# First products of 56 expert tiles instead of 48 ahead of the main loop of a sparse-expert layer

## The chip, the cores and the metric

One core of a Trainium2 chip runs the whole program. The metric is device time in microseconds of one execution, as the median of the runs shown. The engines are TensorE (PE; PEld is its weight load), VectorE (DVE), ScalarE (ACT), GpSimd (POOL) and SyncE (SP). Two queues carry nearly all transfers: the one that SP issues on (the page calls it q1, hardware_dynamic) and the one that POOL's gathers use (q0, software_dynamic). Both share 16 DMA engines.

## The reference, cut to what matters

The layer ends in an expert mixer with 16384 experts, of which each of 1024 tokens picks 8 x 16 = 128 with weights `g`:

```python
a = jnp.einsum('cd,ced->ce', hc, u[ic])          # first product, with u of the picked experts
a = jax.nn.gelu(a, approximate=False) * gc       # gate
return jnp.einsum('ce,ced->cd', a, v[ic])        # second product, with v of the picked experts
```

Before it come projections, two attentions and a memory attention, all in float32; the change touches none of them.

## The kernel before, in words

The tokens are 8 blocks of 128. Blocks 0 to 3 are done **gathered**: for each of their 128 picks POOL gathers 128 rows of `peer_u` (line 1028) or `peer_v` (line 1044), 512 KB, into one of 7 `rows` buffers, and DVE multiplies and sums one such tile (line 1031 for u, line 1050 for v). That is 4 x 2 x 128 = 1024 items, in the order U0 V0 U1 V1 U2 V2 U3 V3. Blocks 4 to 7 are done **dense**: all 16384 experts in 128 tiles of 128 experts, on PE, with a dense weight matrix `Wd` that is zero where an expert was not picked.

`dense` (line 1183) does the dense half in three pieces.

1. **Weights.** The generator `weights` (line 1109) makes `Wd` block by block: a routing (`route`, DVE), codes, and 32 units of two matmuls of codes, a compare on DVE (`ah`, line 1163), a ScalarE step (`oh`, line 1161), four matmuls and a copy to `wbuf` (line 1169). Every 16 units a `wbuf` of 4 MB is full, and 8 stores of 512 KB carry it to `Wd` in DRAM (line 1177).
2. **First products beside it.** For the tiles `e` below `early` (48), `first(e)` (line 1201) loads 512 KB of transposed `peer_u` (`uraw`, 3 buffers), splits it into two float32r parts (ACT writes the high part, line 106; DVE the low part, line 107), and makes 24 matmuls into an `acc` tile. ACT takes the Gelu (line 1217), and SP stores 256 KB as `ga[e]` in DRAM (line 1219). After the last one `pace.drain("weights")` (line 1220) issues whatever of the weights is left.
3. **The main loop**, 32 groups of four tiles. `group` (line 1232) loads `wl` from `Wd` (512 KB for two tiles, line 1237), takes `c` either from `ga` (line 1241, one buffer of 256 KB) or by a fresh `first(e)` and a Gelu (line 1244), multiplies them on DVE (line 1245) and splits the product (ACT and DVE, lines 106 and 107). `second` (line 1251) loads and splits four tiles of `peer_v` (line 1256) and makes 8 sets of 12 matmuls; four sets stay in PSUM (`kept`), four are added to `accu` by DVE (line 1274). So groups 0 to 11 load their `c`, and groups 12 to 31 make it.

The order is set in two steps. `Pace` (line 44) interleaves the generators: each `first` ticks 8 x 3 x 0.216 = 5.184 us and each of the 8 sets of a `second` ticks 2.592 us, and the lane of the gathered items issues one item per `u_each` of ticks (1.3 beside the weights, 2.0 in the main loop, `U_EACH`). Then a list scheduler at build time gives each engine a fixed order by priority: the gathered items stand 3000 instructions behind the place where they were issued (`EXPERT_LAG`), so they fill DVE where the dense work leaves it free. Every engine and the SP queue then run their list strictly in order.

The pools matter too. `gelu`, `wbuf` and the rest of the weights' tiles lie in pool `wb`, which closes before pool `sp` (`wl`, `c`, `v`, `vraw`, `accu`) opens in the same place; and PSUM is laid out anew between them (4 `acc` buffers before, 2 after, beside the four `kept`).

Of the kernel before, what the change touches and what calls it, by code (L numbers as in the profile page):

```python
# [78 lines left out]
class K:  # L79
# [1103 lines left out]
    def dense(self, psum, early):  # L1183
# [5 lines left out]
        with ExitStack() as ctx:  # L1189
# [11 lines left out]
            def first(e):  # L1201
                uT = load_u(e)
                o = self.acc()
                for k in range(KD):
                    self.mm3(o, [u[:, k] for u in uT], [x[:, k] for x in h3], k == 0, k == KD - 1)
                self.pace.tick(KD * 3 * 0.216)
                return o

            ga = {}
            with ExitStack() as c2:  # L1210
                self.wb = c2.enter_context(self.pool("wb"))
                self.u_each = U_EACH[-2]
                self.pace.add("weights", self.weights(blks))
                for e in range(early):
                    o = first(e)
                    t = self.wb.tile([P, 512], F32, name="gelu", bufs=2)
                    nc.scalar.activation(t, o, AF.Gelu)
                    ga[e] = self.scratch([P, 512], f"ga{e}")
                    nc.sync.dma_start(ga[e], t)
                self.pace.drain("weights")  # L1220
            self.route_ctx.close()
            psum = self.psum_phase(psum, "ps3", A_BUFS)
            kept = {}
# [72 lines left out]
    def run(self, ctx):  # L1296
# [74 lines left out]
        psum = self.psum_phase(psum, "ps2", D_BUFS)  # L1371
        psum = self.dense(psum, EARLY)
        self.pace.drain("experts")
        psum.close()


EARLY = 48
V_AHEAD, V_EACH = 0, None
ORDER = [("U", 0), ("V", 0), ("U", 1), ("V", 1), ("U", 2), ("V", 2), ("U", 3), ("V", 3)]
ROWS_T, LOADS_T, FILL_EACH, FILL_LAG = (5, 4), (2, 2), (0.7, 2.4), 100  # L1380
# [5 lines left out]
KEEP, A_BUFS, O_BUFS = 4, 2, 2  # L1386
U_BUFS, V_BUFS = 3, (4, 4, 4)
SELECT_EACH = (5.0, 7.0)
U_EACH, ROUTE_EACH = (1.9, 1.8, 1.9, 1.3, 2.0), 3.0
ROUTE_LAG, EXPERT_LAG = 300, 3000  # L1390
_INS = ["x", "mem", "positions", "norm_mix_g", "w_in", "da_lambda", "da_subln_g", "w_branch_a", "w_branch_b", "gate_bias",
        "w_out", "norm_mem_g", "mem_kv_norm_g", "w_mem_q", "w_mem_kv", "w_mem_o", "norm_ffn_g", "peer_w_q",
# [29 lines left out]
```

## Time and profile before

| | us |
|---|---|
| median of 3 runs | 3506.32 (3500.16 to 3507.83) |
| the profiled execution, its time | 3504.34 |
| its span, first to last instruction | 3502.6 |
| PE busy | 3011.4 |
| DVE busy | 2853.1 |

So 1.7 us of the profiled execution lie outside its span, and it is 2.0 us below the median. Stretches of the trace are given in us from the span's start. The weights and the first products beside them run from about 1640 to 2198, the main loop from 2242 to the end.

### The profile page before, as it was taken

The numbers are of one execution on the slowest core, as the hardware profiler recorded it, in microseconds if no ns is written. First come the engines' busy times: TensorE is split into PE (matmuls) and PEld (weight loads), VectorE is DVE, ScalarE is ACT, GpSimd is POOL, SyncE is SP. The second block draws the span as 40 slices with busy tenths as digits, with TensorE's granted clock in tenths as the row PEclk, the third lists the DMA queues.
The fourth block names the chain that finished last, engine by engine and source line by source line (L and its number), as shares of the span: only waits on it lengthen the run. The fifth ranks groups of instructions, "written<-read, shape, count | busy, mean of one in ns | idle before, by whom it ended". The sixth has DMA issues, their size and how long they took to land. (4 is left out here: it accounts for less than half of the span.)

```text
span 3502.6 us, 42276 instructions
## 1 busy us (share of the span) xinstructions
PE 3011.4 (86%) x13234; PEld 2283.0 (65%) x13234; DVE 2853.1 (81%) x6623; ACT 1398.2 (40%) x2537; POOL 1389.4 (40%) x1122
## 2 busy tenths in 40 slices
PE   8999888798687698676899895588899999999997
PEld 7777766553355575455677674466677888787886
DVE  6656554598878979888999888677789999899998
ACT  5756344245666441322546465222222222222222
POOL 0010000011245246653122665424457665777665
PEclk9999989899899799788999998799999999999999
DMA  4575544335799579897486999999999999999997
GB/s 138 163 186 133 169 138 142 124 121 192 210 296 297 143 262 362 296 327 277 149 296 219 364 377 346 369 302 319 307 340 368 380 381 367 364 364 387 376 381 285
DMA packets 394210, 964.64 MB, mean 275 GB/s; under 512 B 36713, under 2 KB 146049, under 8 KB 392577
## 3 DMA queue, kind: packets, MB, share of 16 engines
q0 software_dynamic: 155264, 560.01, 45.3%
q1 hardware_dynamic: 238720, 401.94, 33.7%
q8 instruction: 104, 1.70, 0.2%
q14 instruction: 122, 0.99, 0.1%
HBM read 871.64 MB, written 90.18 MB: 275 GB/s over the span
## 5 line engine op out<-in xcount | busy, mean ns | idle before, releaser
L1028 POOL DMA_INDIRECT rows<-in_peer_u_dram,ii x512 | 673.8, 1316 | 920.8 <-DVE rows L1031 377.0
L1044 POOL DMA_INDIRECT rows<-in_peer_v_dram,ii x512 | 651.0, 1272 | 438.9 <-DVE h3s L1050 286.2
L1050 DVE SCALAR_TENSOR_TENSOR h3s<-rows,wexp,h3s 128x1024 f32<-128x1024 f32 x508 | 651.1, 1282 | 38.9 <-DMA rows<-in_peer_v_dram,ii 29.4
L1031 DVE SCALAR_TENSOR_TENSOR rows<-rows,h3s 128x1024 f32<-128x1024 f32 x512 | 611.9, 1220 | 81.5 <-DMA rows<-in_peer_u_dram,ii 80.0
L129 PE MATMUL acc<-fT,uT 128*128 128x512 f32 x1024 | 415.7, 406 | 46.3 <-ACT uT L106 26.0
L131 PE MATMUL acc<-fT,uT 128*128 128x512 f32 x1024 | 413.5, 404 | 11.8 <-DVE uT L107 11.5
L130 PE MATMUL acc<-fT,uT 128*128 128x512 f32 x1024 | 410.2, 401 | 0.0
L106 ACT ACTIVATE c<-wl 128x512 fp32r<-128x512 f32 x128 | 80.2, 631 | 817.1 <-PE out L130 407.8
L143 POOL TENSOR_TENSOR rstd<-msq,mhalf 128x1 f32<-128x1 f32 (+1 forms) x42 | 35.6, 847 | 597.4 <-DVE msq L141 578.6
L129 PEld LDWEIGHTS acc<-fT,uT 128*128 128x128 f32 x1024 | 197.0, 192 | 92.2 <-ACT uT L106 26.8
L131 PEld LDWEIGHTS acc<-fT,uT 128*128 128x128 f32 x1024 | 197.0, 192 | 66.7 <-DVE uT L107 21.0
L130 PE MATMUL kept<-v,c 128*128 128x512 f32 x512 | 206.2, 405 | 38.8 <-DVE v L107 38.8
L129 PE MATMUL kept<-v,c 128*128 128x512 f32 x512 | 202.6, 402 | 37.6 <-ACT v L106 36.2
L106 ACT ACTIVATE uT<-uraw 128x1024 fp32r<-128x1024 f32 x128 | 135.5, 1059 | 245.4 <-PE acc L130 135.0
L130 PEld LDWEIGHTS acc<-fT,uT 128*128 128x128 f32 x1024 | 197.2, 193 | 39.2
L107 DVE TENSOR_TENSOR w<-wraw,w 128x512 fp32r<-128x512 f32 (+1 forms) x176 | 116.7, 680 | 117.9 <-ACT w L106 111.2
L129 PE MATMUL out<-v,c 128*128 128x512 f32 x512 | 203.9, 398 | 9.7 <-DVE accu L1274 9.7
L131 PE MATMUL kept<-v,c 128*128 128x512 f32 x512 | 203.4, 397 | 0.0
L130 PE MATMUL out<-v,c 128*128 128x512 f32 x512 | 203.0, 396 | 0.0
L131 PE MATMUL out<-v,c 128*128 128x512 f32 x512 | 202.8, 396 | 0.0
L562 ACT ACTIVATE junk<-W,xb 128x384 bf16<-128x384 f32 (+5 forms) x186 | 163.8, 881 | 77.3 <-DVE xb L560 67.8
L127 PE MATMUL acc<-wraw,hT 128*128 128x512 f32 (+1 forms) x384 | 168.4, 592 | 14.1 <-ACT tok L349 10.9
(361 smaller groups left out, 6691.5 us busy)
## 6 DMA issues: line engine op xcount, KB each, us to landing
uraw<-in_peer_ut_dram SPq DMA_DIRECT2D x128, 512.0 KB
vraw<-in_peer_v_dram SPq DMA_DIRECT2D x128, 512.0 KB
Wd<-wbuf SPq DMA_DIRECT2D x64, 512.0 KB
wl<-Wd SPq DMA_DIRECT2D x64, 512.0 KB
wraw<-in_w_in_dram SPq DMA_DIRECT2D x40, 512.0 KB
fraw<-in_w_in_dram SPq DMA_DIRECT2D x32, 512.0 KB
wraw<-in_w_out_dram SPq DMA_DIRECT2D x24, 512.0 KB
ga<-gelu SPq DMA_DIRECT2D x48, 256.0 KB
```

The costliest lines, as they stand in the source:

```text
L106: self.nc.scalar.activation(hi, src, AF.Copy)
L107: self.last_dve = self.nc.vector.tensor_tensor(lo, src, hi.bitcast(F32), op=OP.subtract).ins
L127: self.last_pe = nc.tensor.matmul(out, l[0], r[0], start=start, stop=stop).ins
L129: nc.tensor.matmul(out, l[0], r[0], start=start, stop=False)
L130: nc.tensor.matmul(out, l[0], r[1], start=False, stop=False)
L131: self.last_pe = nc.tensor.matmul(out, l[1], r[0], start=False, stop=stop).ins
L143: nc.gpsimd.tensor_tensor(r, v, self.mhalf[:, :n], op=OP.pow)
L562: nc.scalar.activation(junk[:, :(b + 1) * P], self.W[b], AF.Sign, bias=xb[:, j:j + 1].bitcast(F32), accum_out=s[:, j:j + 1])
L1028: nc.gpsimd.indirect_dma_start(out=u, out_offset=None, in_=a["peer_u"][0], in_offset=bass.IndirectOffsetOnAxis(ap=ii[:, j:j + 1], axis=0))
L1031: nc.vector.scalar_tensor_tensor(u, u, 1.0, h3, op0=OP.mult, op1=OP.mult, accum_out=aa[:, j:j + 1])
L1044: nc.gpsimd.indirect_dma_start(out=v, out_offset=None, in_=a["peer_v"][0], in_offset=bass.IndirectOffsetOnAxis(ap=r["ii"][:, j:j + 1], axi ...
L1050: nc.vector.scalar_tensor_tensor(o, v, w[:, j:j + 1], o, op0=OP.mult, op1=OP.add)
```

## The change

It makes and stores the first products of 56 tiles instead of 48, so that groups 12 and 13 load their `c` as well. `drain("weights")` stays where it was, behind tile 47; the eight further tiles come behind it, inside the same loop and before the pool `wb` closes. And the pace of the gathered items in the main loop is 1.95 instead of 2.0.

```diff
@@ -1217,7 +1217,8 @@
                     nc.scalar.activation(t, o, AF.Gelu)
                     ga[e] = self.scratch([P, 512], f"ga{e}")
                     nc.sync.dma_start(ga[e], t)
-                self.pace.drain("weights")
+                    if e == BESIDE - 1:
+                        self.pace.drain("weights")
             self.route_ctx.close()
@@ -1374,7 +1375,7 @@
-EARLY = 48
+EARLY, BESIDE = 56, 48
@@ -1386,7 +1387,7 @@
-U_EACH, ROUTE_EACH = (1.9, 1.8, 1.9, 1.3, 2.0), 3.0
+U_EACH, ROUTE_EACH = (1.9, 1.8, 1.9, 1.3, 1.95), 3.0
```

## Rows read from the trace of the kernel before

**Rows 1.** The page's busy times, and its 40 slices of the span (87.6 us each), in tenths.

```profile
PE 3011.4 (86%) x13234; PEld 2283.0 (65%) x13234; DVE 2853.1 (81%) x6623; ACT 1398.2 (40%) x2537; POOL 1389.4 (40%) x1122
...
PE   8999888798687698676899895588899999999997
...
DVE  6656554598878979888999888677789999899998
```

**Rows 2.** Busy time of each engine in five stretches: the end of the weights, the passage to the main loop, the main loop up to group 11 (4th product of group 0 to 4th product of group 11), groups 12 to 30, and the end. Columns: stretch, length, busy us of the engines (instructions), granted TensorE clock, DMA share, GB/s.

```profile
2118.00:2198.00 80.00, 56.17 (x342) 43.92 (x343) 74.47 (x91) 54.88 (x70) 49.66 (x41) 0.88 0.92 335
2198.00:2242.00 44.00, 10.09 (x45) 8.05 (x44) 24.28 (x22) 4.88 (x7) 19.08 (x18) 0.66 1.03 392
...
2255.00:2549.00 294.00, 242.50 (x950) 190.39 (x949) 225.66 (x308) 67.69 (x90) 106.02 (x87) 0.91 0.92 310
2549.00:3443.00 894.00, 870.77 (x3774) 713.04 (x3773) 847.15 (x1036) 244.78 (x318) 596.65 (x434) 0.99 0.99 370
3443.00:3502.60 59.60, 41.03 (x180) 33.31 (x178) 50.42 (x51) 12.58 (x19) 26.76 (x22) 0.88 0.74 264
```

**Rows 3.** The same columns for two stretches of 100 us, one where the gathered items are v and one where they are u.

```profile
2800.00:2900.00 100.00, 100.00 (x443) 82.80 (x442) 98.66 (x96) 27.23 (x35) 66.12 (x50) 1.00 1.02 382
3100.00:3200.00 100.00, 95.70 (x414) 78.45 (x413) 91.82 (x142) 28.69 (x37) 72.28 (x50) 0.98 0.98 363
```

**Rows 4.** PE in order of time around the passage: first and last of the 48 matmuls of tiles 48 and 49, and the first matmuls of group 0. Columns: start, us, engine, line, what; in brackets the idle time before it and what ended it.

```profile
2196.69 0.47 PE L129 MATMUL acc<-fT,uT 128*128 128x512 f32 x1
...
2207.47 0.39 PE L131 MATMUL acc<-fT,uT 128*128 128x512 f32 x1
2241.77 0.79 PE L129 MATMUL kept<-v,c 128*128 128x512 f32 x1 [33.91 <-ACT v L106]
2242.36 0.63 PE L129 MATMUL out<-v,c 128*128 128x512 f32 x1
...
2245.88 0.43 PE L129 MATMUL out<-v,c 128*128 128x512 f32 x1
```

**Rows 5.** The SP queue in order of time from 2116 to 2245: its transfers as issued, in its fixed order.

```profile
2116.64 0.33 SPq L1196 DMA_DIRECT2D uraw<-in_peer_ut_dram  x1
2118.46 0.33 SPq L1219 DMA_DIRECT2D ga<-gelu  x1
2120.49 0.33 SPq L1196 DMA_DIRECT2D uraw<-in_peer_ut_dram  x1
2164.78 43.63 SPq L1177 DMA_DIRECT2D Wd<-wbuf  x16
2208.51 6.34 SPq L1196 DMA_DIRECT2D uraw<-in_peer_ut_dram  x2
2214.95 1.16 SPq L1237 DMA_DIRECT2D wl<-Wd  x1
2216.16 5.05 SPq L1241 DMA_DIRECT2D c<-ga  x1
```

**Rows 6.** The DMA queues from 2198 to 2242: packets, MB, share of the 16 engines.

```profile
q0 software_dynamic: 2454, 8.92, 51.6%
q1 hardware_dynamic: 4206, 8.30, 51.4%
...
rows<-in_peer_v_dram,ii POOLq DMA_INDIRECT x18
```

**Rows 7.** DVE in order of time: the product of the gate and the weights of a tile (line 1245), first of group 0, then the 4th of groups 0, 11 and 30.

```profile
2237.51 0.69 DVE L1245 TENSOR_TENSOR wl<-c,wl 128x512 f32<-128x512 f32 x1 [10.02 <-DMA c<-ga]
...
2255.04 0.69 DVE L1245 TENSOR_TENSOR wl<-c,wl 128x512 f32<-128x512 f32 x1 [1.37 <-DMA c<-ga]
...
2549.07 0.69 DVE L1245 TENSOR_TENSOR wl<-c,wl 128x512 f32<-128x512 f32 x1 [1.39 <-DMA c<-ga]
...
3442.84 0.68 DVE L1245 TENSOR_TENSOR wl<-acc,wl 128x512 f32<-128x512 f32 x1
```

**Rows 8.** DVE's groups of instructions from 2255 to 2549 (groups 1 to 11): count, busy us, mean ns, and the idle time before them with what ended it.

```profile
L1031 DVE SCALAR_TENSOR_TENSOR rows<-rows,h3s 128x1024 f32<-128x1024 f32 x56 | 66.3, 1220 | 2.8 <-DMA rows<-in_peer_u_dram,ii 2.8
...
L1050 DVE SCALAR_TENSOR_TENSOR h3s<-rows,wexp,h3s 128x1024 f32<-128x1024 f32 x29 | 37.1, 1280 | 0.1
L1245 DVE TENSOR_TENSOR wl<-c,wl 128x512 f32<-128x512 f32 x44 | 30.4, 692 | 62.7 <-DMA c<-ga 37.3 <-DMA wl<-Wd 17.6 <-issue 7.5
```

**Rows 9.** The same from 2549 to 3443 (groups 12 to 30).

```profile
L1050 DVE SCALAR_TENSOR_TENSOR h3s<-rows,wexp,h3s 128x1024 f32<-128x1024 f32 x232 | 297.4, 1282 | 10.0 <-DMA rows<-in_peer_v_dram,ii 5.3
L1031 DVE SCALAR_TENSOR_TENSOR rows<-rows,h3s 128x1024 f32<-128x1024 f32 x200 | 237.4, 1221 | 35.9 <-DMA rows<-in_peer_u_dram,ii 35.0 <-DMA h3s<-h 0.7
...
L107 DVE TENSOR_TENSOR uT<-uraw,uT 128x1024 fp32r<-128x1024 f32 x76 | 92.5, 1217 | 0.9 <-ACT uT L106 0.9
...
L1048 DVE TENSOR_SCALAR h3s<-rows,wexp 128x1024 f32<-128x1024 f32 x2 | 1.5, 753 | 0.1
```

**Rows 10.** Who waited for whom on PE from 2549 to 3443: us in total, times, longest.

```profile
PE acc L129 <- DVE wl L1245: 20.2, 10, 4.3
```

## The prediction

> **What bounds the kernel now.** I read the page's busy times and slices first, for where engines stand idle together; then the table by stage; then PE, SP and DVE in order of time around the one hole that the table shows; last the groups of instructions of the main loop's two halves. In the slices PE and DVE are near 9 only from slice 30 on [rows 1]. In the table [rows 2] the reader is to see three regimes. From 2549 on PE has 871 of 894 us and DVE 847: both are nearly full, and which one sets the pace changes with the gathered items: with v items PE is full and DVE at 98.7, with u items both have holes [rows 3], the largest of PE's being 20.2 us behind DVE's product [rows 10]. From 2255 to 2549, where groups load their `c`, PE has 242 of 294 us and DVE 226; DVE waits 62.7 us at line 1245, 37.3 of them for the single `c` buffer's load [rows 8]. And from 2198 to 2242 PE has 10 of 44 us and DVE 24 [rows 2]: PE ends tile 49 at 2207.7 and starts group 0 33.9 us later [rows 4]. In that passage the transfers are what is late. SP stood from 2121 to 2165 waiting for a `wbuf` to fill, then pushed 16 stores in 43.6 us, two loads of `uraw`, and only at 2215 the first `wl` [rows 5]; the gathers and SP's queue each took 51% of the 16 engines, 392 GB/s together [rows 2, 6]. The first product of group 0 ran at 2237.5, after DVE had waited 10.0 us for its `c` [rows 7].
>
> **The change, part by part.** The sum is against the profiled execution, 3504.34 us; the median is 2.0 higher.
>
> (a) *Groups 12 and 13 change kind.* A group that loads took (2549.07 - 2255.04) / 11 = 26.7 us, one that makes its `c` (3442.84 - 2549.07) / 19 = 47.0 [rows 7]. Two of them: 2 x 20.3 = 40.6 us less. This counts everything these groups lose (8 `uraw` loads, 8 splits on ACT and DVE, 192 matmuls) and gain (8 `c` loads in the one-buffer chain), and it counts the gathered items that go with them, for which see (c).
>
> (b) *The eight first products come ahead of group 0.* PE needs 11.0 us for two [rows 4], so 44.0 for eight. The hole is 33.9, so PE alone would start group 0 10.1 later; that is the lower end, if tiles 56 and 57 are run ahead into the two `acc` buffers as 48 and 49 were. Past the SP queue go 8 loads of 0.52 MB and 8 stores of 0.26 MB, 6.3 MB, ahead of `wl`. If they only add to the common 392 GB/s they cost 16.0 us; at the rate that SP's queue itself had, 8.30 MB in 44 us = 189 GB/s [rows 6], 33.3, the upper end. I take 13, between PE's 10.1 and 16.0: two of the loads already stand ahead of the stores [rows 5], and SP has 44 empty us there for one more. In the hole PE falls to its lower clock: the granted clock of the stretch is 0.66 [rows 2], and the first matmuls of group 0 stand 0.44 us apart against 0.23 before it [rows 4], some 2 us over the ten of them. A filled hole gives these back: -2.
>
> The eight Gelus (ACT is at a third or less in the main loop [rows 2]) cost nothing; their cover is ACT's idle time, and if it went they would delay only the stores, 0.6 us each. The passage adds one wait: SP's store of `ga` waits for its Gelu, and queued behind it are the loads of `wl`, `c` and `vraw` that group 0 waits for; that is the slower rival below.
>
> (c) *The gathered items lose their place.* A group that loads carried 85 / 11 = 7.7 items, one that makes carried (232 + 2 + 200) / 19 = 22.8 [rows 8, 9]. Two that change kind drop 30.2 items. A passage 13 us longer takes 13 x 18 / 44 = 5.3 of them at the rate the gathers had there [rows 6]; 24.9 are left, at 1.28 us [rows 9] 31.9 us of DVE. Nothing hides them in full: where items are v, DVE is at 98.7 of 100 [rows 3]. Against them stand DVE's 10.0 us at the first `c` [rows 7], which eight first products give the load time to cover, and u items that move out of the late groups, where each waits (35.0 / 200) 0.17 us for its rows, against 0.05 in the groups that load [rows 8, 9]: two more such groups with some ten u items each, 2.4 us. I take 31.9 - 12.4 = 19.5. The bounds are 0 (the late groups' 47 us of DVE idle [rows 2] take all) and 31.9.
>
> (d) *The pace.* The eight firsts tick 41.5 us, so 31.9 items are issued ahead of the main loop; its ticks fall from 1078 to 1037 us, at 1.95 instead of 2.0, so 532 instead of 539 items. The list thus runs out 24 items, about one group, sooner. POOL's queue gets these gathers earlier, but each waits for a `rows` buffer that DVE frees, and DVE's order is filled by what room the dense work leaves: 22 to 24 items in a late group, 8 in a loading one, not the 20.7 and 10.4 that the pace of 2.0 asks for [rows 8, 9]. I take 0; ends -5 (the end of the list no longer trails the last group) and +5.
>
> Sum: -40.6 + 13 - 2 + 19.5 + 0 = -10.1. The profiled execution would take 3494.2, the median 3496.2.
>
> **A rule that speaks against it.** In the passage both queues are always pending and share evenly, 51.6 against 51.4% [rows 6]. The Trainium skill, "DMA: Bandwidth & Descriptors", section "Queues, rings and completion order", says that each DMA engine takes turns between the queue rows with work, a packet at a time. By it SP's queue could not get more than its even share while gathers are waiting, (b) would be 33.3 and not 13, and the sum +10 before the longer passage is credited with its items; the trace agrees with the even split, but not that gathers are pending all through a longer passage, which no run here shows.
>
> **The rivals.**
>
> *No change.* Follow DVE instead of PE. Its work is the same in both kernels, so only its idle time counts: from 2198 on 19.7 us in the passage, 68.3 in the groups that load, 46.9 after, 9.2 at the end [rows 2]. Two more groups of the loading kind add 2 x 6.2 = 12.4; two fewer of the other kind save 2 x 2.5 = 4.9; the passage keeps its 20, since gathers there come every 44 / 18 = 2.4 us. Net +7 at most, and -3 if the 10.0 us at the first `c` go: 3503 to 3513. For it: DVE's 98.7 [rows 3]. Against it: PE's waits for DVE in the late groups are only 20 us [rows 10].
>
> *Slower: SP's queue.* The eighth `ga` store stands ahead of the first `wl`, and from the issue of that `wl` to group 0 took 2241.8 - 2215.0 = 26.8 us [rows 4, 5], with 16 stores just ahead. If SP's list has the loads of group 0 behind the last Gelu, the hole is not filled but pushed behind the eight: (b) is 33 instead of 13. The longer passage takes 13.5 items, 16.7 are left, 21 us. Sum: -40.6 + 33 + 21 = +13, 3519. It decides the sign once group 0 starts later than 2241.8 + 20.
>
> *Much faster.* All items find room: -40.6 + 10.1 + 0 = -30, 3476. Against it rows 3.
>
> *The change doesn't do what it says.* PE has 24 idle us in the weights' last 80 [rows 2]; the builder may order the eight into these gaps instead of behind the last unit. DVE is at 74.5 of 80 there, so eight splits of 1.22 [rows 9] push its items out, and the hole stays with its wait for the stores. (b) is then 0 to 5, but the 10.0 us of (c) stay: -40.6 + 3 + 29 = -9, the same time by another way; it is counted with the forecast.
>
> **How the numbers follow.** About 0.2% (7 us) is what a measurement of this kernel can tell from no change. The forecast (3485 to 3499) has 0.36, with the last rival in it; much faster 0.08; no change 0.34; slower 0.22. So faster 0.44, same 0.34, slower 0.22. The likeliest case's own range is 3485 to 3499; to leave out no more than 2 in 10 the range reaches into the faster case to 3480 and over the slower one's 3519, to 3520.
>
> **What would show it.** Right: group 0's first matmul between 2250 and 2260 with a hole of under 10 us before it, groups 12 and 13 at some 27 us, and groups 14 to 30 at 47 to 49. PE's hole behind tile 55 still over 25 us: the SP rival. Late groups at 49 us or more with DVE at 98% and PE's waits for DVE's product well over 20 us: no change. It is wrong altogether if stretches before 2118 move by more than a few us, since nothing in the sum touches them, or if the loading groups slow from 26.7 because more u items fall into them.

## The result, and the profile after

The median went from 3504.7 us (4 runs) to 3529.2 us (4 runs, 3521.5 to 3534.6): a ratio of 1.0058, 95% interval 1.0036 to 1.0080, which is 13 to 28 us slower. I had forecast 3496 with a range of 3480 to 3520, and gave slower 0.22. The profiled execution of after, the shortest of its four, took 3521.47 us with a span of 3519.7, so the two profiles show 17 us of the 24 between the medians.

The busy times and the PE and DVE slices of after, to be laid beside [rows 1]:

```profile
PE 3011.1 (86%) x13234; PEld 2279.9 (65%) x13234; DVE 2855.8 (81%) x6623; ACT 1395.1 (40%) x2537; POOL 1370.1 (39%) x1122
...
PE   8999888798687698686899889788889999999991
...
DVE  6656444698878889888999789687789999899997
```

The instructions are as many on every engine, and PE's, DVE's and ACT's busy times are the same to about 3 us. PE's hole behind the weights is smaller (slices 25 and 26 were 5 and 5, now 9 and 7) and PE's last slice fell from 7 to 1, while DVE goes on at 7. The table by stage of after, to compare with [rows 2] (columns as there; the stretches begin and end at the same marks of the program):

```profile
2118.00:2198.00 80.00, 77.08 (x463) 59.54 (x462) 75.25 (x93) 60.58 (x79) 45.27 (x38) 1.00 0.94 350
2198.00:2245.00 47.00, 27.54 (x109) 21.48 (x107) 28.27 (x24) 8.82 (x11) 19.95 (x18) 0.81 1.03 395
2256.00:2548.00 292.00, 244.69 (x977) 193.41 (x976) 224.99 (x302) 67.81 (x90) 103.93 (x86) 0.93 0.92 317
2548.00:2610.00 62.00, 50.16 (x193) 39.43 (x192) 45.91 (x71) 12.19 (x16) 25.24 (x19) 0.89 0.88 297
2610.00:3404.00 794.00, 777.26 (x3374) 637.09 (x3373) 757.00 (x935) 220.07 (x286) 526.24 (x387) 0.99 1.00 372
3404.00:3447.00 43.00, 42.90 (x190) 35.08 (x188) 42.37 (x39) 6.85 (x10) 30.16 (x26) 1.00 0.88 309
3447.00:3519.70 72.70, 0.30 (x2) 0.00 (x0) 52.53 (x47) 5.63 (x10) 31.11 (x31) 0.52 0.74 276
```

The last four stretches in before, cut at the 4th product of groups 13 and 31 and at PE's last matmul:

```profile
2549.00:2625.00 76.00, 73.47 (x316) 60.20 (x315) 70.60 (x108) 21.61 (x28) 44.97 (x34) 0.97 0.94 339
2625.00:3443.00 818.00, 797.30 (x3460) 652.84 (x3459) 776.54 (x929) 223.18 (x290) 551.67 (x401) 0.99 1.00 373
3443.00:3483.60 40.60, 40.60 (x179) 33.30 (x178) 36.90 (x37) 9.13 (x13) 23.32 (x19) 1.00 0.85 305
3483.60:3502.60 19.00, 0.43 (x2) 0.01 (x1) 13.52 (x15) 3.45 (x6) 3.44 (x3) 0.63 0.48 174
```

Read the lengths: 76 became 62, 818 became 794, and the end behind PE's last matmul went from 19.0 to 72.7. There DVE's busy time is 52.5 where it was 13.5.

The eight first products stand mostly inside the weights' drain: PE starts six of them between 2114 and 2195 and the other two by 2206. Tiles 56 and 57 then run ahead of group 0, as 48 and 49 did in before; the matmuls at 2228.59 to 2236.72 are tile 57's. PE's waits ahead of group 0, beside [rows 4]:

```profile
2228.59 0.79 PE L129 MATMUL acc<-fT,uT 128*128 128x512 f32 x1 [11.52 <-ACT uT L106]
...
2236.72 0.39 PE L131 MATMUL acc<-fT,uT 128*128 128x512 f32 x1
2245.15 0.80 PE L129 MATMUL kept<-v,c 128*128 128x512 f32 x1 [8.04 <-ACT v L106]
2245.74 0.63 PE L129 MATMUL out<-v,c 128*128 128x512 f32 x1
2246.17 0.63 PE L129 MATMUL kept<-v,c 128*128 128x512 f32 x1
```

SP's queue over the same time, beside [rows 5]; seven of the eight stores of `ga` are out by 2210, before, between or right behind the stores of `wbuf`, the eighth at 2223.65:

```profile
2155.86 0.33 SPq L1219 DMA_DIRECT2D ga<-gelu  x1
2158.14 0.33 SPq L1196 DMA_DIRECT2D uraw<-in_peer_ut_dram  x1
2162.59 9.24 SPq L1177 DMA_DIRECT2D Wd<-wbuf  x8
...
2197.44 9.08 SPq L1177 DMA_DIRECT2D Wd<-wbuf  x8
2206.62 2.98 SPq L1219 DMA_DIRECT2D ga<-gelu  x2
...
2223.65 0.32 SPq L1219 DMA_DIRECT2D ga<-gelu  x1
2224.06 0.86 SPq L1196 DMA_DIRECT2D uraw<-in_peer_ut_dram  x2
2225.02 0.40 SPq L1238 DMA_DIRECT2D wl<-Wd  x1
```

The 4th products of groups 0, 11, 13 and 31 on DVE, beside [rows 7] (group 13 stood at 2625.27 in before, group 31, the last, at the 3442.84 shown there):

```profile
2256.07 0.69 DVE L1246 TENSOR_TENSOR wl<-c,wl 128x512 f32<-128x512 f32 x1 [0.43 <-DMA c<-ga]
...
2547.79 0.69 DVE L1246 TENSOR_TENSOR wl<-c,wl 128x512 f32<-128x512 f32 x1 [1.41 <-DMA c<-ga]
...
2609.81 0.69 DVE L1246 TENSOR_TENSOR wl<-c,wl 128x512 f32<-128x512 f32 x1 [1.29 <-DMA c<-ga]
...
3404.06 0.69 DVE L1246 TENSOR_TENSOR wl<-acc,wl 128x512 f32<-128x512 f32 x1 [0.17 <-ACT acc L1245]
```

And the end on DVE, in order of time from PE's last matmul (3446.91) on; below it the last item and the last instruction of before:

```profile
3447.94 27.70 DVE L1050 SCALAR_TENSOR_TENSOR h3s<-rows,wexp,h3s 128x1024 f32<-128x1024 f32 x21
...
3489.89 1.28 DVE L1050 SCALAR_TENSOR_TENSOR h3s<-rows,wexp,h3s 128x1024 f32<-128x1024 f32 x1 [2.81 <-DMA rows<-in_peer_v_dram,ii]
3492.40 1.28 DVE L1050 SCALAR_TENSOR_TENSOR h3s<-rows,wexp,h3s 128x1024 f32<-128x1024 f32 x1 [1.23 <-DMA rows<-in_peer_v_dram,ii]
3493.72 1.22 DVE L1063 TENSOR_TENSOR rows<-rows,h3s 128x1024 f32<-128x1024 f32 x1
...
3514.81 1.28 DVE L148 SCALAR_TENSOR_TENSOR uraw<-uraw,rstd,vraw 128x1024 f32<-128x1024 f32 x1 [0.73 <-POOL rstd L143]
```

```profile
3492.47 1.28 DVE L1050 SCALAR_TENSOR_TENSOR h3s<-rows,wexp,h3s 128x1024 f32<-128x1024 f32 x1
...
3497.64 1.28 DVE L148 SCALAR_TENSOR_TENSOR rows<-rows,rstd 128x1024 f32<-128x1024 f32 x1 [0.73 <-POOL rstd L143]
```

PE is done 37 us sooner, but the last gathered item starts at 3492.40, in before at 3492.47. Behind it come the finish of gathered block 3 and the finishes of the four dense blocks (a finish adds the residual, normalizes and stores a block); in before the dense finishes began among the items. Items behind group 31's products: 56, in before 22.

### The profile page after: what moved, and what is told of

Read it like the earlier page. It is cut to its first block, busy times and chain, and to the rows that moved or that the text cites. A ratio compares the mean times of both kernels' runs of the same rounds, so it can differ in the third digit from the quotient of the medians.

```text
span 3519.7 us, 42272 instructions
## 1 busy us (share of the span) xinstructions
PE 3011.1 (86%) x13234; PEld 2279.9 (65%) x13234; DVE 2855.8 (81%) x6623; ACT 1395.1 (40%) x2537; POOL 1370.1 (39%) x1122
## 4 chain that ended last, share of the span: by engine, by line
PE 31%; DVE 20%; issue 19%; DMA 15%; POOL 10%; ACT 5%; SPq 0%; POOLq 0%; ACTq 0%; DVEq 0%
POOL rows L1028 6%; PE acc L129 4%; PE acc L130 4%; PE acc L131 4%; POOL rows L1044 4%; DMA c<-ga 3%; DMA rows<-in_peer_u_dram,ii 3%; PE po L720 2%; DVE h3s L1050 2%; DVE rows L1031 2%; DMA rows<-in_peer_v_dram,ii 2%; DMA so<-pq 2%; PE fill L127 1%; PE acc L127 1%; PE out L1167 1%
## 5 line engine op out<-in xcount | busy, mean ns | idle before, releaser
L1028 POOL DMA_INDIRECT rows<-in_peer_u_dram,ii x512 | 666.1, 1301 | 947.1 <-DVE rows L1031 407.7
L1044 POOL DMA_INDIRECT rows<-in_peer_v_dram,ii x512 | 643.5, 1257 | 451.2 <-DVE h3s L1050 291.7
L1050 DVE SCALAR_TENSOR_TENSOR h3s<-rows,wexp,h3s 128x1024 f32<-128x1024 f32 x508 | 651.4, 1282 | 37.1 <-DMA rows<-in_peer_v_dram,ii 26.9
```

The costliest lines, as they stand in the source:

```text
L1028: nc.gpsimd.indirect_dma_start(out=u, out_offset=None, in_=a["peer_u"][0], in_offset=bass.IndirectOffsetOnAxis(ap=ii[:, j:j + 1], axis=0))
L1044: nc.gpsimd.indirect_dma_start(out=v, out_offset=None, in_=a["peer_v"][0], in_offset=bass.IndirectOffsetOnAxis(ap=r["ii"][:, j:j + 1], axi ...
L1050: nc.vector.scalar_tensor_tensor(o, v, w[:, j:j + 1], o, op0=OP.mult, op1=OP.add)
```

## The experiments

Times are medians; ratios are against runs of before on the same chip, in brackets the 95% interval. All profiles begin to differ by some us in the stages that nothing touches (the first split of `uT`, with which the weights' stage begins, starts between 1631 and 1645), so stages are compared by their lengths.

**Is it the pace?** The change also set the pace from 2.0 to 1.95. One run undoes that, one does it alone.

```
e1_pace20 (of after):      U_EACH[-1]  1.95 -> 2.0
e2_pace_only (of before):  U_EACH[-1]  2.0  -> 1.95
```

> The changed kernel with the pace of the gathered items back at 2.0. Theory (order of the finishes): the main loop's ticks, 1036.8 us, still issue 518 items at 2.0, and only 511 are left behind the eight, so the list still runs out inside the loop, the finish of gathered block 3 is still issued ahead of the finishes of the dense blocks, and ScalarE's and DVE's lists still hold those back behind the last item: the tail of 20 us stays, 3520 to 3532, like the changed kernel. Rival (the pace of 1.95 itself costs the time): back to the kernel before, 3500 to 3508.

> The kernel before with the pace 1.95 alone, 48 early tiles. Theory (order of the finishes): 1078.3 us of ticks issue 553 items and only 542 are left, so the list runs out inside the loop and the four dense finishes queue up behind the gathered one; PE ends near 3485 as before, the last item near 3485 to 3490, then about 20 us of finishes one after the other: 3508 to 3518. Rival (the eight tiles cost the time, not the pace): within 5 us of the kernel before.

e1: 3534.0, ratio 1.0088 [1.0064, 1.0112], 2 us above the range of its theory. e2: 3505.3 in 10 runs (3491 to 3525), 1.0004 [0.9986, 1.0022], as its rival had it. The pace alone is worth nothing that can be measured, and undoing it in after gives nothing back; term (d) stands.

**Is it the order of the finishes at the end?** In after the finish of the gathered block 3 stands ahead of the dense ones, which then run one behind the other for 20 us. e3 issues it behind them; e4 lets the list of items outlast the loop. (The edits are cut to what matters, here and below.)

```
e3_held:     gathered_v, block 3:  self.held = (b, o); return   # instead of finish
             run, after the drain: self.finish(*self.held, ...)
e4_pace205:  U_EACH[-1]  1.95 -> 2.05
```

> The changed kernel, with the finish of gathered block 3 held back and issued behind the dense finishes. Theory: the last item stays near 3494, since DVE's work sets it, but the dense finishes run between PE's end (3447) and 3475, and only one finish of 6 to 9 us comes behind the last item: 3498 to 3508, equal to the kernel before, with PE done 35 us earlier. Rival (the tail is slow because its gathers are, not for the order): within 5 us of the changed kernel, 3520 or more.

> The changed kernel with the pace at 2.05: 1036.8 / 2.05 = 506 items are issued in the loop and 511 are left, so the list does not run out and the last finish is issued behind the dense ones, with no other edit. Theory (order of the finishes): as e3, 3498 to 3508. Rival (a thinner pace lets more items pile up behind PE's end): slower than the changed kernel, 3530 or more.

e3: 3522.4, 1.0059 [1.0038, 1.0080]. e4: 3526.0, 1.0068 [1.0044, 1.0093]. The theory fell (e4 lies below its rival's 3530, too). In e3's trace the dense finishes do run among the items, and the last item starts at 3517.8 instead: the finishes cost their time in either place.

**Is it the number of items?** The last 36 v items of block 3 left out, in after and in before, each with block 3's finish held as in e3.

```
e5_held_short, e6_before_held_short:  for j in range(P - 36 if b == NG - 1 else P)
```

> The changed kernel with the finish of gathered block 3 held back as before, and the last 36 of its 128 v items left out (the sums of block 3 lack them). Theory (DVE's ledger: with the eight tiles PE is done 35 to 40 us early and what is left is the items that had no place, one after the other at 1.3 us): 36 x 1.32 = 47 us less than the held kernel's 3522, 3470 to 3482, and PE ends again near 3450 to 3460. Rival (PE and its finishes still set the end): within 10 us of 3522.

> The kernel before with the same two edits: the last 36 v items of block 3 left out. Theory (DVE's ledger): in the kernel before PE and the items end together, so PE's end near 3484 and the finishes behind it hold the time: 3490 to 3502, at most 10 us less than the kernel before. Rival (items set the end there too): 3455 to 3465.

e5: 3472.1, 0.9896 [0.9871, 0.9921], 50 us under e3. e6: 3499.9, 0.9987 [0.9976, 0.9997], 2 us under before. Both as expected: items set the end of after, while in before PE's dense work is late enough to hide 36 of them. With 36 items fewer in both, the change gains 28 us (3472.1 against 3499.9), so PE's gain is real; the items eat it.

**DVE's additions, or the gathers?** An item is both, so e5 could not tell. e13 leaves the last 36 gathers and cuts their additions to 8 columns; e14 leaves the additions and takes the gathers away. Both are edits of after with the finish held.

```
e13: scalar_tensor_tensor(o[:, :8], v[:, :8], ...)        # last 36 items
e14: if not last 36:  v = self.rows(); indirect_dma_start(out=v, ...)
```

> The kernel after with block 3's finish held (as in the run named held), and of the last 36 v items of block 3 only the gathers stay: their DVE additions are cut from 1024 columns to 8, so their sums are incomplete in the other columns. 36 x 1.28 = 46 us of DVE work leave, no gather does. DVE theory (DVE's work alone sets the end): 3470 to 3484, as when both were left out (3472.1). Gathers theory (behind PE's end GpSimd issues the gathers back to back, one per 1.02 + 0.30 = 1.32 us, and DVE follows them): 3510 to 3522, against 3522.35 with all of it. Something between, 3490 to 3505: DVE sets the pace up to PE's end and the gathers behind it.

> The other half of the same test: the last 36 v items of block 3 keep their full DVE additions but have no gather of their own (they add the last gathered rows again, so the sums of block 3 are other ones). 36 x 1.32 = 47.5 us of GpSimd's issuing and 18.9 MB of transfers leave, no DVE work does. DVE theory: 3510 to 3522. Gathers theory, and one by which the transfers' bytes set the end (18.9 MB at 372 GB/s are 51 us): 3470 to 3484. In between, 3490 to 3505: the two limit together.

e13: 3520.8, 1.0063 [1.0044, 1.0082]. e14: 3521.8, 1.0058 [1.0039, 1.0077]; 10 runs each, against 3522.4 for e3. Taking away either half alone is worth nothing, both together 50 us. The stretch behind PE's end, first e13, then e14 (columns as in the table by stage):

```profile
3453.00:3516.60 63.60, 0.46 (x3) 0.03 (x1) 14.88 (x40) 3.45 (x6) 30.37 (x32) 0.55 0.83 308
```

```profile
3458.00:3521.40 63.40, 0.69 (x4) 0.23 (x2) 52.71 (x45) 3.45 (x6) 3.52 (x3) 0.54 0.11 41
```

Same length, 63.6 and 63.4 us, with DVE busy 14.9 in one and 52.7 in the other, and 308 against 41 GB/s. What each runs at, GpSimd's gathers in e13 and DVE's additions in e14, in order of time:

```profile
3496.72 0.94 POOL L1044 DMA_INDIRECT rows<-in_peer_v_dram,ii  x1 [0.30 <-issue]
3497.96 0.93 POOL L1044 DMA_INDIRECT rows<-in_peer_v_dram,ii  x1 [0.30 <-issue]
```

```profile
3470.46 39.58 DVE L1051 SCALAR_TENSOR_TENSOR h3s<-rows,wexp,h3s 128x1024 f32<-128x1024 f32 x30
3510.08 1.22 DVE L1067 TENSOR_TENSOR rows<-rows,h3s 128x1024 f32<-128x1024 f32 x1
```

A gather takes GpSimd 1.24 us (the starts' distance), an addition 39.58 / 30 = 1.32 us of DVE, alone on its engine in both cases. So behind PE's end an item costs 1.3 us twice, side by side, and only fewer items make it shorter. That the two lengths agree so well is partly chance: in e13 the dense finishes stand among the last gathers, and GpSimd waits 5.2 and 2.3 us for DVE's part of two of them.

**How does it go with the number of early products?** e11 and e15 make 64 and 40 of them; e12 moves the drain, so that all 56 stand beside the weights.

```
e11_early64:         EARLY, BESIDE = 64, 48      # of after
e12_beside56:        EARLY, BESIDE = 56, 56      # of after
e15_before_early40:  EARLY = 40                  # of before
```

> The changed kernel with 64 early tiles instead of 56, so that groups 14 and 15 load their c too. Theory (DVE's ledger): PE ends another 25 to 40 us earlier, some 30 more items are left behind its end, two more loading groups add 10 us of DVE idle time and the longer tail some 3 to 5: 3538 to 3548. Rival (the 25 us are a fixed price of breaking the order at the passage): 3500 to 3525, the 40 us of PE coming back.

> The changed kernel with the weights drained behind all 56 tiles, as the loop of the kernel before does with its 48: the same work, the eight not behind the drain but beside it. Theory (DVE's ledger: where PE does the eight is of no account): within 8 us of the changed kernel, 3520 to 3537. Rival (the place behind the last unit is what costs, by its loads and stores at the passage): back to 3500 to 3512.

> The kernel before with 40 early first products, not 48: the change run backwards. Theory of two ends (PE's dense work and the items end together in the kernel before; whichever is later sets the time): PE's end moves back by 2 x 20.3 = 40.6 us and the items gain room, so PE sets the end: 3530 to 3548. Rival (what more early products cost comes on top whatever PE does, so fewer of them gain): 3478 to 3495.

e11: 3555.8, 1.0145 [1.0121, 1.0169], 8 us above what I expected. e12: 3521.0, 1.0059 [1.0038, 1.0081]: where the eight are put does not matter, as expected. In e12's trace PE's hole is back, and group 0 starts 626.9 us behind the first split instead of 606.2:

```profile
2269.29 0.79 PE L129 MATMUL kept<-v,c 128*128 128x512 f32 x1 [34.48 <-ACT v L106]
```

PE ends 13.7 us later than in after by that measure, and the end behind it is 50.4 us instead of 72.4: PE's later end costs nothing.

e15: 3502.3, 1.0007 [0.9986, 1.0028], a miss for both theories. I had PE's end moved back by 40.6 us, but the weights' stage became 46 us shorter too (434.4 instead of 480 us from the first split to 80 us ahead of the last `wbuf`) and the passage behind it 12 us, while PE's main loop became only 31 us longer; PE ended 27 us sooner against the first split, and 16 items started behind its end (3 in before). So before does not stand at a sharp crossing; from 40 to 48 the time is flat, and by the ratios it rises by about 20 us to 56 and by 30 more to 64.

One row of each tells why: the stretch from the first split of `uT` to the end, in the order 40, 48 (before), 56 (after), 64:

```profile
1640.00:3501.10 1861.10, 1665.16 (x7496) 1337.20 (x7496) 1656.29 (x2935) 638.77 (x826) 970.92 (x732) 0.95 0.91 331
```

```profile
1637.00:3502.60 1865.60, 1659.84 (x7496) 1330.39 (x7496) 1654.88 (x2935) 639.33 (x825) 969.14 (x732) 0.95 0.91 333
```

```profile
1638.90:3519.70 1880.80, 1658.61 (x7496) 1328.09 (x7496) 1658.04 (x2935) 637.32 (x825) 949.05 (x732) 0.95 0.91 332
```

```profile
1641.70:3567.70 1926.00, 1674.77 (x7496) 1340.14 (x7494) 1660.60 (x2936) 636.93 (x825) 952.50 (x732) 0.93 0.90 327
```

DVE's busy time is 1655 to 1661 in all four; what is left of the length, its idle time, is 204.8, 210.7, 222.8 and 265.4. In e11 the second eight don't fit into the drain: its passage is 103 us long with DVE at 71.5 of it, and two more groups wait for their `c`. (e11's profiled execution is 14 us over its median.)

**Two ways to make items cheaper or waits fewer.** A second `c` buffer should end the 37.3 us of [rows 8]; and GpSimd could take a quarter of the late groups' splits of `v` off DVE.

```
e7 (of before), e8 (of after, finish held):  name="c", bufs=1 -> 2
e9 (of after), e10 (of before), from group 14 on, last tile of a group:
   nc.scalar.activation(vv[0], raw, AF.Copy)
   nc.gpsimd.tensor_tensor(vv[1], raw, vv[0].bitcast(F32), op=OP.subtract)
```

> The kernel before with two buffers for the loaded c instead of one. Theory (DVE's idle time counts one for one): DVE's 50 us of waiting for c's load and part of the 18 for wl go, 20 to 45 us less: 3455 to 3482. Rival (the loading groups are held by the transfers, or by PE): within 7 us of the kernel before.

> The changed kernel with two buffers for the loaded c and the finish of gathered block 3 held back. Theory (DVE's ledger): 56 loads now go unwaited for, 25 to 50 us less than the held kernel's 3522, and the eight tiles then cost no more than 5 us against the kernel before with two buffers: 3460 to 3495. Rival (transfers hold the loading groups): within 7 us of 3522.

> The changed kernel with one of the four v splits of each group from 14 on taken from DVE and given to GpSimd (18 subtractions of 128x1024). Theory (DVE's ledger: behind PE's end DVE still has 36 items, so DVE's work counts one for one): 18 x 1.14 = 20 us of DVE go, 17 items fewer behind PE's end, 3502 to 3514 against 3529 for the changed kernel. Rival (GpSimd's own queue or the gathers set the end): within 7 us of 3529, or slower, as its subtraction delays gathers.

> The kernel before with the same 18 subtractions given to GpSimd. Theory (PE and DVE end together there): PE's end near 3484 holds the time, at most 8 us less: 3492 to 3502. Rival (DVE alone sets the end before, too): 3480 to 3487.

The theory missed in all four. e7: 3507.9, 1.0010 [0.9996, 1.0025], as its rival had it; e8: 3536.6, 1.0079 [1.0054, 1.0105], outside both, though not clear of e3's 1.0059. DVE's waits in e7's loading groups (total us, times, longest):

```profile
DVE wl L1245 <- DMA wl<-Wd: 29.4, 6, 8.2
DVE wl L1245 <- issue: 12.0, 3, 6.0
DVE wl L1245 <- DMA c<-ga: 11.4, 5, 4.0
DVE accu L1274 <- PE out L131: 9.6, 10, 2.0
```

The wait mostly changed its name: for `c` 11.4 instead of 37.3, for `wl` 29.4 instead of 17.6, at "issue" 12.0 instead of 7.5 [rows 8], and for PE's `out` 9.6 instead of 2.5. A second buffer of `c` alone does not shorten these groups.

e9: 3545.7, 1.0112 [1.0086, 1.0139], slower, as its rival allowed; e10: 3518.2, 1.0055 [1.0034, 1.0076], outside both. The splits of `v` that stay on DVE, from 2620 to 3420, in after and in e9 (count, busy us, mean ns):

```profile
L107 DVE TENSOR_TENSOR v<-vraw,v 128x1024 fp32r<-128x1024 f32 x72 | 84.1, 1218 | 0.0
```

```profile
L107 DVE TENSOR_TENSOR v<-vraw,v 128x1024 fp32r<-128x1024 f32 x52 | 95.5, 1877 | 0.0
...
L1260 POOL TENSOR_TENSOR v<-vraw,v 128x1024 fp32r<-128x1024 f32 x18 | 44.2, 2455 | 5.9 <-ACT v L1259 5.6
```

Twenty splits fewer stand in the window (18 of them on GpSimd), and the others take 11.4 us more than all 72 did; the last section shows how.

## Why the prediction was wrong, point by point

(a) *Two groups change kind*: right. From group 0's first matmul to its last matmul, PE took 1241.8 us in before and 1201.8 in after, 40.0 less; I had 40.6. By the 4th products, groups 12 and 13 took 30.0 and 32.0 us, more than my 27. Group 14 took 27.9 instead of 47.9, as group 12 took 27.1 in before: two of its first products stand ahead of group 0.

(b) *The eight ahead of group 0*: mis-sized. I had +13 - 2; against the first split, group 0's first matmul moved by 1.4 us (604.8 to 606.2). My last rival described it: the eight went into the gaps of the drain, where PE is now busy for 77.1 of 80 us instead of 56.2, and of the 33.9 us of the passage some 20 are still idle (11.5 and 8.0 above). The 6.3 MB cost nothing that shows. The -2 for the clock did not come: behind the hole of 8.0 us group 0's first matmuls stand 0.43 us apart again, and the granted clock from 2245.1 to 2250.0 is 0.50, the lower of the two levels. The Trainium skill's rule that a DMA engine takes turns between the queues with work ("DMA: Bandwidth & Descriptors", "Queues, rings and completion order"), by which (b) would have been 33.3, did not decide. The shares were even again, 52.3 and 50.6% from 2198 to 2245, but most of the transfers had gone out earlier instead of waiting in the passage. The slower rival had the right sign and the wrong mechanism.

(c) *The gathered items*: the step that failed. I took 31.9 us for 24.9 items and credited 12.4; the end behind PE's last matmul grew by 53.8 us against the 19.5 of the term. Three things were wrong in it. First, 34 more items were left behind group 31's products (56 against 22), not 24.9. Groups 12 to 14 carried 31 instead of 59, near my 30.2, but no longer passage took any: up to group 0's 4th product 478 items were done, in before 483, with eight more splits on DVE ahead of group 0. Second, the credits: the wait for the first `c` went from 10.0 to 1.2 us, but DVE idles 18.7 us in the passage where it did 19.7, now for ACT's part of `uT` (8.5 us) and the second `c`. Only the u items' shorter waits may have come: DVE's idle time from group 13 to 31 fell from 41.5 to 37.1. Third, and what I had not seen at all: behind PE's end items have no dense work beside them to fill their waits, so the end is a serial chain of items at 1.3 us each and the finishes. From PE's last matmul to the end of the last addition it is 46.8 us (10.2 in before), and from there to the end of the span 26.0 (8.8). e5 shows that the items are the cause, e13 and e14 that neither of their two halves is it alone.

(d) *The pace*: 0 was right (e1, e2).

The sum from the first split to the end: +1.4 - 40.0 + 53.8 = +15.2, which is the difference of the two rows above (1880.8 - 1865.6). The rival that should have been the forecast is *no change*: it followed DVE, whose work is constant, and only its idle time counts. It gave at most +7, since it took DVE's idle time behind PE's end as constant; that went from 5.5 to 20.2 us, and in groups 12 and 13 from 5.3 to 16.1, while all other stages together lost some 13. Of the 16.1, 15.3 are the waits at line 1246 that come with a loading group:

```profile
L1246 DVE TENSOR_TENSOR wl<-c,wl 128x512 f32<-128x512 f32 x9 | 6.2, 690 | 15.3 <-DMA wl<-Wd 10.5 <-DMA c<-ga 4.7
```

My argument against it, that PE waits for DVE only 20 us in the late groups, proves nothing: it says that PE is full there, not that what DVE puts off is free. The late groups' reading of PE as the bound was right and useless: room on PE is worth something only if the items fit into the shorter time.

Two readings in the prediction are slightly off: in slices 21 and 22 both engines are at 9 as well, and tile 49 ends at 2207.86, which adds 0.7 us to (b). Neither matters.

What stays open: how the 20 to 24 us of the medians divide between the two more loading groups and the end, since no run separates them. The sums of single profiles move as much as they differ: e2's profiled execution, 20 us over its median, has 221 us of DVE idle time. The places hold, though. In groups 12 and 13 DVE idles 12 to 16 us in the profiles of e1, e3, e4 and e12, with 56 tiles, and 6 to 8 in those of e2 and e7, with 48; behind PE's last matmul it is 14 to 20 against 5 to 12. No version was found that beats before.

## What to carry to other kernels

Where a filler list of constant work runs beside the engine that looks full, make the sum on the filler's engine too, stage by stage and up to the very end: count how many fillers the shortened stage will no longer carry, and price them at the rate at which they run alone. A gain of one engine that only moves its end away from the other's is no gain, and an item that costs two engines the same can't be made cheaper on one of them. The way to see it beforehand is one run with some fillers left out: here 36 of them were worth 2 us in one kernel and 50 in the other.

## What the runs showed of the hardware

- GpSimd's subtraction and DVE's don't run beside each other. In e9 two splits of `v` on DVE that meet GpSimd's take 5.04 us, where 2 x 1.22 = 2.4 were usual; the difference, 2.6, is about GpSimd's own 2.4. At each of GpSimd's 18 subtractions the DVE instruction beside it is longer by 1.9 to 2.7 us:

```profile
2718.84 2.40 POOL L1260 TENSOR_TENSOR v<-vraw,v 128x1024 fp32r<-128x1024 f32 x1
```

```profile
2718.42 5.04 DVE L107 TENSOR_TENSOR v<-vraw,v 128x1024 fp32r<-128x1024 f32 x2
```

  The Trainium skill says so ("SBUF — State Buffer", "Who interferes with whom"): a DVE instruction with two inputs in SBUF contends with a GpSimd instruction that reads SBUF, and the ports that they share are an exclusive lock. The trace agrees that one is held for the other's whole length. Which came first it can't tell: DVE's record begins 0.42 us ahead of GpSimd's, and yet DVE is the one that is held.
- With the gathers out of the way (e14, 41 GB/s) a DVE addition took 1.32 us per item, and beside them (after, 276 GB/s) 27.70 / 21 = 1.32 us, so the transfers don't slow it.
